# Values and gates of the first 512 tokens behind the first layer's last product

## The chip, the cores and the metric

The program runs on one core of a Trainium2 chip. The metric is the device time of one execution in microseconds. A profile shows the time of each engine: TensorE (PE; its weight loads are PEld), VectorE (DVE), ScalarE (ACT), GpSimd (POOL), and SyncE (SP), whose queue issues the transfers from and to device memory.

## The reference

One layer of an encoder on two sequences, 1024 tokens ("sample") and 512 ("prompt"), width 1024, hidden width 2816, all in float32:

```python
x = x + 0.5 * rmsnorm(swiglu(rmsnorm(x, g0), w1, w3, w2), g1)      # first layer (ffn1), post-norm
h = rmsnorm(x, mix_pre_g)                                          # x / sqrt(mean(x^2) + 1e-6) * g
u = h @ w_in                                                       # 1024 -> 3584 columns
hyena: u[:, :1536], short_conv: up[:L] * w[0] + up[1:L+1] * w[1] + up[2:] * w[2] + b, then two
       long convolutions with filters from hyena_filters() (an MLP with sin over the positions)
retention: q, k = rotary(heads(u[:, 1536:2048])), rotary(heads(u[:, 2048:2560])),
       v = heads(u[:, 2560:3072]), g = u[:, 3072:3584]; silu(g) * rmsnorm(retention(q, k, v))
x = x + rmsnorm(concat(hyena, retention) @ w_out, mix_post_g)
x = x + 0.5 * rmsnorm(swiglu(rmsnorm(x, ...), ...), ...)           # second layer (ffn2)
```

## The kernel before, in words

**Numbers.** A float32 product is made of three matmuls in a rounded format: each operand is split into a high and a low part (hi x hi, hi x lo, lo x hi). `mm3` (L67 to L69) issues the three, `hi_act` (L59) makes a high part on ScalarE as a copy, `lo` (L62) the low part as a difference on the engine that it is given. So each weight block costs a load on SyncE, a high on ScalarE and a low on VectorE or GpSimd before TensorE can use it.

**Stages.** All 1536 tokens lie as columns. `ffn` takes them in two groups of 768, each in two halves (th) of 384. `up_unit` and `down` make the hidden layer and its product by block schemes with fewer products; the weights are loaded as `raw` tiles. At the program's start `normed` loads x in four quads (xq, L192), squares them on ScalarE (L156), sums on VectorE, makes row sums on TensorE (ss, L170 in `rstd3`), the factor r, and spreads it over the partitions by three transposes (rps, L177 in `spread`); only then can the first product start. At the end of each group `post_quads` does the same to the output z: r is spread, z is scaled (L403), the residual is added (L404), z is stored as x1 to device memory, squared and summed, and the row of factors for the next norm goes to device memory (row1, L411).

Behind ffn1 come: `norm_T` (L115), which loads x1 and the row of factors (L122) for 512 tokens, scales (L129) and splits them to hh and hl; `w_in_v` (L813), the values of 512 tokens with four weight chunks (raw2, w2h, w2l), evicted by VectorE (vo, L835); and `w_in_pass` (L774), 24 blocks of 128 columns: 0 to 11 for hyena with the short convolution (its factors are in scw), 12 to 19 queries and keys with rotation, 20 to 23 the gates with silu. It takes tokens 0 to 1023 at once, and beside it `filter_mlp` (products fps, L695) and `filter_taps` (products tapps, L723 and L724; their eviction L725) make the long filters. The values of tokens 512 to 1023 follow, then retention with the last 512 tokens, the long convolutions, the output product and the second layer.

**Order.** `gen_run(main, side, rate)` interleaves two generators in the source. The order on each engine is then set at build time by a planner that simulates the engines (`schedule_with_timeline_sim=True`), so that the program's order is not the source's. A pool hands a buffer out again as soon as its last reader is done. On one engine, and in SyncE's queue, instructions issue in order: what stands behind a waiting one waits too.

The lines that the change replaces: `mix_in_consts` (L840) loads scw and the rotation's tables ahead of the pass; L1235 opens the ffn with its own PSUM pool; the low parts of the first `norm_T`, of `w_in_v` and of `w_in_pass` are made by GpSimd.

## Time and profile before

| | us |
|---|---|
| median of 3 runs | 3313.13 |
| lowest and highest | 3307.2, 3317.64 |
| the profiled execution | 3313.05 |
| its span | 3311.3 |
| TensorE busy in the span | 3068.8 (93%) |
| VectorE busy | 2591.7 (78%) |
| ScalarE busy | 1518.8 (46%) |
| GpSimd busy | 518.1 (16%) |

The profile counts an engine as busy while it executes, not while it waits or issues. A wait is put down to the instruction that came last by its semaphore. The granted clock (PEclk) is TensorE's, as a share of the upper one of its two levels, 1.2 and 2.4 GHz. Transfers run on 16 shared engines, whose mean busy share is the DMA share.

### The profile page before, as it was taken

What the parts mean: (1) busy time and instruction counts of PE and PEld (TensorE: products, weight loads), DVE (VectorE), ACT (ScalarE), POOL (GpSimd) and SP (SyncE); (2) the same over time, 40 slices, a digit from 0 to 9 for tenths busy, and PEclk for the clock granted to TensorE, in tenths of its full rate; (3) what the DMA queues carried; (4) which work ended last, traced back from release to release, by engine and by line L of the source; (5) the groups of instructions that cost most, each with busy time, mean ns of one, the idle gap of its engine ahead of it and who ended that gap; (6) DMA issues with size and microseconds to landing.
All of it is one profiled execution on the core that took longest, in us unless ns stands there. A gap on an engine that the chain in (4) does not pass through costs nothing. (4 is left out here: it accounts for less than half of the span.)

```text
span 3311.3 us, 46272 instructions
## 1 busy us (share of the span) xinstructions
PE 3068.8 (93%) x16764; PEld 2884.0 (87%) x16764; DVE 2591.7 (78%) x4211; ACT 1518.8 (46%) x2588; POOL 518.1 (16%) x380
## 2 busy tenths in 40 slices
PE   5999999999898899989997998896899999999997
PEld 5999999999898677768787887775899999999997
DVE  8888788876786499777676878877889788867776
ACT  6333455433455344457544344455433456433454
POOL 0000000000200322356333534530000000000000
PEclk8999999999999899999998998997899999999998
DMA  3676344422344624444544124465778354322344
GB/s 132 245 297 226 88 151 134 124 71 70 102 118 146 189 105 154 159 168 143 175 115 154 45 85 165 136 200 155 252 262 315 105 150 153 125 74 74 84 130 137
DMA packets 223028, 489.51 MB, mean 148 GB/s; under 512 B 37456, under 2 KB 65488, under 8 KB 220624
## 3 DMA queue, kind: packets, MB, share of 16 engines
q1 hardware_dynamic: 222800, 486.57, 45.1%
q8 instruction: 131, 2.15, 0.3%
q14 instruction: 97, 0.79, 0.1%
HBM read 384.70 MB, written 101.75 MB: 147 GB/s over the span
## 5 line engine op out<-in xcount | busy, mean ns | idle before, releaser
L68 PE MATMUL dn<-xl,w2h 128*128 128x384 f32 x1232 | 416.6, 339 | 6.3 <-DVE xl L62 6.3
L59 ACT ACTIVATE wh<-s 128x512 fp32r<-128x512 f32 x352 | 221.4, 631 | 417.4 <-PE ua L68 115.5
L67 PE MATMUL dn<-xh,w2h 128*128 128x384 f32 x1232 | 404.7, 339 | 0.1
L69 PE MATMUL dn<-xh,w2l 128*128 128x384 f32 x1232 | 403.4, 338 | 0.0
L59 ACT ACTIVATE wh<-raw 128x512 fp32r<-128x512 f32 (+1 forms) x312 | 216.7, 694 | 348.5 <-PE ub L68 92.9
L59 ACT ACTIVATE w2h<-raw 128x512 fp32r<-128x512 f32 (+1 forms) x340 | 228.3, 672 | 301.8 <-PE dn L68 191.7
L62 DVE TENSOR_TENSOR wl<-s,wh 128x512 fp32r<-128x512 f32 x352 | 241.4, 687 | 159.6 <-ACT wh L59 88.2
L95 POOL TENSOR_TENSOR r<-m,mhalf 128x3 f32<-128x3 f32 (+1 forms) x35 | 43.1, 1232 | 1875.9 <-DVE m L94 1874.5
L62 DVE TENSOR_TENSOR w2l<-raw,w2h 128x512 fp32r<-128x512 f32 (+1 forms) x316 | 221.6, 710 | 107.4 <-ACT w2h L59 92.0
L67 PE MATMUL wips<-hh,wh 128*128 128x512 f32 x576 | 233.2, 405 | 15.8 <-DVE vo L835 7.6
L68 PEld LDWEIGHTS dn<-xl,w2h 128*128 128x128 f32 x1232 | 233.1, 189 | 7.1 <-DVE xl L62 7.0
L69 PE MATMUL wips<-hh,wl 128*128 128x512 f32 x576 | 232.6, 404 | 2.2 <-POOL wl L62 2.2
L68 PE MATMUL wips<-hl,wh 128*128 128x512 f32 x576 | 232.4, 404 | 0.5 <-POOL hl L62 0.5
L67 PEld LDWEIGHTS dn<-xh,w2h 128*128 128x128 f32 x1232 | 231.7, 189 | 0.6 <-ACT xh L59 0.4
L69 PEld LDWEIGHTS dn<-xh,w2l 128*128 128x128 f32 x1232 | 232.1, 189 | 0.0
L62 DVE TENSOR_TENSOR wl<-raw,wh 128x512 fp32r<-128x512 f32 (+1 forms) x276 | 196.6, 712 | 24.8 <-ACT wh L59 23.1
L67 PE MATMUL fw<-th,mh 128*128 128x256 f32 x448 | 131.8, 296 | 31.1 <-DVE spec L924 21.0
L67 PEld LDWEIGHTS wips<-hh,wh 128*128 128x128 f32 x576 | 111.5, 194 | 44.4 <-ACT hh L59 11.7
L67 PE MATMUL ub<-t2h,wh 128*128 128x384 f32 x352 | 120.8, 343 | 28.9 <-ACT t2h L59 24.5
L69 PEld LDWEIGHTS wips<-hh,wl 128*128 128x128 f32 x576 | 111.1, 193 | 29.7 <-POOL wl L62 2.9
L68 PEld LDWEIGHTS wips<-hl,wh 128*128 128x128 f32 x576 | 111.4, 193 | 28.0 <-POOL hl L62 1.1
L68 PE MATMUL fw<-tl,mh 128*128 128x256 f32 x448 | 132.5, 296 | 0.3 <-DVE tl L62 0.2
(384 smaller groups left out, 9082.2 us busy)
## 6 DMA issues: line engine op xcount, KB each, us to landing
raw<-ffn_w SPq DMA_DIRECT2D x440, 256.0 KB, 2.7
raw<-ws SPq DMA_DIRECT2D x220, 256.0 KB, 2.7
wsum<-ffn_w SPq DMA_DIRECT2D x60, 768.0 KB, 7.2
raw<-w_in_f SPq DMA_DIRECT2D x48, 512.0 KB, 4.3
ws<-wsum SPq DMA_DIRECT2D x30, 768.0 KB, 6.1
xq<-x SPq DMA_DIRECT2D x16, 768.0 KB, 5.9
res<-x SPq DMA_DIRECT2D x16, 768.0 KB, 6.2
wsum<-ffn_w SPq DMA_DIRECT2D x20, 512.0 KB, 7.0
```

The lines of the kernel that those rows point to most:

```text
L59: self.nc.scalar.activation(hi, src, AF.Copy)
L62: eng.tensor_tensor(lo, src, hi.bitcast(F32), ALU.subtract)
L67: mm(ps, lhsT=ah, rhs=bh, start=first, stop=False, **kw)
L68: mm(ps, lhsT=ah, rhs=bl, start=False, stop=False, **kw)
L69: mm(ps, lhsT=al, rhs=bh, start=False, stop=last, **kw)
L95: nc.gpsimd.tensor_tensor(r, m, self.mhalf[:, :n], ALU.pow)
```

## The change

The values of tokens 0 to 511 are computed right behind the last product of ffn1, and the gates (blocks 20 to 23) of the same tokens behind them; the row sums of the new x1 come among them, later than before. Two of the four weight chunks of the values are loaded and split beside the last product (`first_values`, in quads of pool yq). The PSUM pool of eight banks stays open over ffn1 and these two products. The gates of tokens 512 to 1023 become a pass of their own. The factors of tokens 768 to 1023 are spread over the partitions by two transposes (`spread(r, 2)`) rather than read back from row1. The low parts of these weights and of the norm of tokens 512 to 1023 go from GpSimd to VectorE where the diff says so (`nc.vector`), and the values are evicted by ScalarE. scw becomes a tile of the setup, loaded by `short_consts`, which the ffn calls.

```diff
@@ -81,6 +81,7 @@
         self.gains = self.cp.tile([128, 6, KD], F32, name="gains")
         nc.sync.dma_start(self.gains, self.io["gains"])
+        self.scw = self.cp.tile([128, NHY, 4], F32, name="scw", bufs=1)
...
@@ -112,14 +113,15 @@
-    def norm_T(self, src, g, gi, hp, row, eng=None):
+    def norm_T(self, src, g, gi, hp, row, eng=None, r=None):
 
 
         nc = self.nc
         hh = hp.tile([128, KD, 512], F32R, tag="hh", name="hh")
         hl = hp.tile([128, KD, 512], F32R, tag="hl", name="hl")
-        r = self.np.tile([128, 512], F32, tag="rpre", name="rrow", bufs=1)
-        nc.sync.dma_start(r, row[:, 512 * g:512 * g + 512].broadcast_to([128, 512]))
+        if r is None:
+            r = self.np.tile([128, 512], F32, tag="rpre", name="rrow", bufs=1)
+            nc.sync.dma_start(r, row[:, 512 * g:512 * g + 512].broadcast_to([128, 512]))
...
@@ -170,10 +172,10 @@
-    def spread(self, r):
+    def spread(self, r, n=3):
 
         ps = self.bank("rps")
-        for t in range(3):
+        for t in range(n):
             self.nc.tensor.transpose(ps[:, t * 128:(t + 1) * 128], r[:, t:t + 1].broadcast_to([128, 128]), self.ident)
         return ps
 
@@ -406,11 +408,12 @@
             if row is not None:
                 acc = self.sum_sq([z[0, th], z[1, th]], Y)
                 yield
-                r = self.rstd3(acc)
+                self.row_r = r = self.rstd3(acc)
                 c = 768 * g + 384 * th
                 nc.sync.dma_start(row[:, c:c + 384].rearrange("o (c p) -> (o p) c", p=128), r)
 
-    def ffn(self, n, srcs, dsts, row_in, row_out, X, Y, lead=None):
+    def ffn(self, n, srcs, dsts, row_in, row_out, X, Y, lead=None, extra=()):
@@ -441,7 +444,8 @@
-            self.pm = own.enter_context(pool("pm", 8, space=PSUM))
+            if not extra:
+                self.pm = own.enter_context(pool("pm", 8, space=PSUM))
...
@@ -465,6 +469,8 @@
                 yield from self.weight_sums(w2, Y)
+                if extra:
+                    extra[0]()
@@ -497,6 +503,8 @@
                     for p, c in self.down(w2, hid, Y, z, (1, 4, 7, 2, 3, 5, 6)):
                         if (p, c) == (6, 0):
                             z["sum"] = self.sum_sq([z[0, 1]], Y)
+                        if extra and (p, c) == (3, 0):
+                            extra[1](Y)
                         if p == 6 or (p, c) == (5, 2):
                             run(post_of)
         self.rest = post_of
@@ -771,13 +779,12 @@
-    def w_in_pass(self, hTs, base, gp, rp, wp, psp, d, blks, eng):
+    def w_in_pass(self, hTs, base, gp, rp, wp, psp, d, blks, eng, tag="wi"):
 
         nc = self.nc
         n = len(hTs)
         W = 512 * n
         cols = slice(base, base + W)
-        cos, sin = (self.rope[:, i, :W] for i in range(2))
...
             self.hi_act(wh, raw)
             self.lo(eng, wl, raw, wh)
-            ps = psp.tile([128, W], F32, tag="wi", name="wips")
+            ps = psp.tile([128, W], F32, tag=tag, name="wips")
@@ -801,6 +808,7 @@
                 sw = gp.tile([128, W], F32, tag="c", name="sw")
                 nc.scalar.activation(sw[0:64], ps[64:128], AF.Copy)
                 nc.scalar.activation(sw[64:128], ps[0:64], AF.Copy)
+                cos, sin = (self.rope[:, i, :W] for i in range(2))
                 nc.vector.tensor_tensor(o, ps, cos, ALU.mult)
                 nc.gpsimd.tensor_tensor(sw, sw, sin, ALU.mult)
...
@@ -810,20 +818,38 @@
-    def w_in_v(self, hT, base, n, gp, rp, wp, psp, d, eng):
+    def first_values(self, Y):
+
+        nc = self.nc
+        self.early = []
+        for k2 in range(2):
+            raw, wh, wl = (self.quad(Y, n, t).rearrange("p a b -> p (a b)")[:, :1024].rearrange("p (j c) -> p j c", c=512)
+                           for n, t in (("raw2", F32), ("w2h", F32R), ("w2l", F32R)))
+            nc.sync.dma_start(raw, self.io["w_in_v"][k2])
+            self.hi_act(wh, raw)
+            self.lo(nc.vector, wl, raw, wh)
+            self.early.append((wh, wl))
+
+    def w_in_v(self, hT, base, n, gp, rp, wp, psp, d, eng, banks=False):
 
         nc = self.nc
         hh, hl = hT
         for t0 in range(0, 4, 2 * n):
-            full = [psp.tile([128, 512 * n], F32, tag="wi", name="v") for _ in range(2)]
-            ps = [full[t // n][:, t % n * 512:t % n * 512 + 512] for t in range(2 * n)]
+            if banks:
+                ps = [psp.tile([128, 512], F32, tag="mm", name="v") for _ in range(2 * n)]
+            else:
+                full = [psp.tile([128, 512 * n], F32, tag="wi", name="v") for _ in range(2)]
+                ps = [full[t // n][:, t % n * 512:t % n * 512 + 512] for t in range(2 * n)]
             for k2 in range(4):
-                raw = rp.tile([128, 2, 512], F32, tag="raw", name="raw2")
-                nc.sync.dma_start(raw, self.io["w_in_v"][k2])
-                wh = wp.tile([128, 2, 512], F32R, tag="w", name="w2h")
-                wl = wp.tile([128, 2, 512], F32R, tag="w", name="w2l")
-                self.hi_act(wh, raw)
-                self.lo(eng, wl, raw, wh)
+                if banks and self.early:
+                    wh, wl = self.early.pop(0)
+                else:
+                    raw = rp.tile([128, 2, 512], F32, tag="raw", name="raw2")
+                    nc.sync.dma_start(raw, self.io["w_in_v"][k2])
+                    wh = wp.tile([128, 2, 512], F32R, tag="w", name="w2h")
+                    wl = wp.tile([128, 2, 512], F32R, tag="w", name="w2l")
+                    self.hi_act(wh, raw)
+                    self.lo(eng, wl, raw, wh)
@@ -832,18 +858,19 @@
                 yield
             for t in range(2 * n):
                 o = gp.tile([128, 512], F32, tag="vo", name="vo", bufs=2)
-                nc.vector.tensor_copy(o, ps[t])
+                self.hi_act(o, ps[t])
                 nc.sync.dma_start(d["v"][base // 128 + t0 + t], o)
             yield
 
-    def mix_in_consts(self, gp, rop):
-        nc = self.nc
-        self.rope = rop.tile([128, 2, 1024], F32, name="rope", bufs=1)
-        nc.sync.dma_start(self.rope, self.io["rope"])
-        self.scw = gp.tile([128, NHY, 4], F32, name="scw", bufs=1)
+    def short_consts(self):
+        nc = self.nc
         for i in range(3):
             nc.sync.dma_start(self.scw[:, :, i], self.io["short_w"][i])
         nc.sync.dma_start(self.scw[:, :, 3], self.io["short_b"])
+
+    def mix_in_consts(self, rop):
+        self.rope = rop.tile([128, 2, 1024], F32, name="rope", bufs=1)
+        self.nc.sync.dma_start(self.rope, self.io["rope"])
@@ -1211,23 +1238,36 @@
         with ExitStack() as right:
             e = right.enter_context
             with pool("yq", 20) as Y:
+                pm1 = ExitStack()
+                self.pm = pm1.enter_context(pool("pm", 8, space=PSUM))
                 with pool("xq", 6, side="right") as X, pool("fs", side="right") as self.fs, pool("ft", 6, side="right") as self.ft, \
                         pool("fw", 10, side="right") as self.fw, pool("fr", 5, side="right") as self.fr:
-                    self.ffn(1, xs, x1, None, row1, X, Y)
+                    self.ffn(1, xs, x1, None, row1, X, Y, extra=(self.short_consts, self.first_values))
                 hp = e(pool("hT", side="right"))
-                with pool("xin", 2, side="right") as self.xp, pool("nrm", side="right") as self.np, \
-                        pool("raw", 2, side="right") as raw, pool("w", 4, side="right") as wp, \
-                        pool("gv", 2, side="right") as gp, pool("ft", 6, side="right") as self.ft, \
-                        pool("wv", 2, space=PSUM) as psw, pool("pm", 2, space=PSUM) as self.pm:
+                near = ExitStack()
+                self.xp, self.np = (near.enter_context(pool(n, b, side="right")) for n, b in (("xin", 2), ("nrm", 1)))
+                with pool("gv", 2, side="right") as gp, pool("ft", 6, side="right") as self.ft, \
+                        pool("w", 4, side="right") as wp, pool("raw", 2, side="right") as raw:
                     hTs = [self.norm_T(x1, 0, 2, hp, row1, nc.gpsimd)]
-                    gen_run(self.w_in_v(hTs[0], 0, 2, gp, raw, wp, psw, d, nc.gpsimd), self.rest, 2)
-            with pool("raw", 2) as raw, pool("w", 4) as wp, pool("scw") as gp, pool("rope") as rop:
-                self.mix_in_consts(gp, rop)
-                self.ret_consts(rop)
-                with pool("g", 4) as gp, pool("nrm") as self.np, pool("xin", 2) as self.xp, pool("hT2") as hp2, pool("wi", 2, space=PSUM) as psw, \
+
+                    def main():
+                        yield from self.w_in_v(hTs[0], 0, 2, gp, raw, wp, self.pm, d, nc.vector, banks=True)
+                        yield from self.w_in_pass(hTs, 0, gp, raw, wp, self.pm, d, range(20, 24), nc.vector, tag="mm")
+
+                    rr = self.np.tile([128, 512], F32, tag="rr", name="rrow", bufs=1)
+                    nc.sync.dma_start(rr[:, :256], row1[:, 512:768].broadcast_to([128, 256]))
+                    for i, _ in enumerate(main()):
+                        for _ in range({1: 2, 2: 2, 7: 2}.get(i, 0)):
+                            next(self.rest, None)
+                        if i == 1:
+                            self.hi_act(rr[:, 256:], self.spread(self.row_r, 2)[:, :256])
+                pm1.close()
+            with pool("raw", 2) as raw, pool("w", 4) as wp, pool("rope") as rop:
+                with near, pool("g", 4) as gp, pool("hT2") as hp2, pool("wi", 2, space=PSUM) as psw, \
                         pool("f", 2) as fp, pool("fps", 2, space=PSUM) as psf:
                     hs = [fp.tile([128, 512], F32R, tag=f"h3_{s}", name="h3", bufs=1) for s in range(3)]
-                    hTs.append(self.norm_T(x1, 1, 2, hp2, row1, nc.gpsimd))
+                    hTs.append(self.norm_T(x1, 1, 2, hp2, row1, nc.vector, rr))
+                    self.mix_in_consts(rop)
 
                     def side():
                         yield from self.filter_mlp(fp, psf, hs)
@@ -1237,7 +1277,9 @@
                     hTp = []
 
                     def main():
-                        yield from self.w_in_pass(hTs, 0, gp, raw, wp, psw, d, range(24), nc.gpsimd)
+                        yield from self.w_in_pass(hTs, 0, gp, raw, wp, psw, d, range(20), nc.gpsimd)
+                        yield from self.w_in_pass(hTs[1:], 512, gp, raw, wp, psw, d, range(20, 24), nc.gpsimd)
+                        self.ret_consts(rop)
                         hTp.append(self.norm_T(x1, 2, 2, hp, row1, nc.gpsimd))
                         yield from self.w_in_v(hTs[1], 512, 2, gp, raw, wp, psw, d, nc.gpsimd)
```

SyncE's queue at the program's start, before: constants, two loads of x, five of weights, two of x, nine of weights.

```order
L75 DMA ident<-ident 128x128
L83 DMA gains<-gains 128x48
L192 DMA xq<-x 128x1536 x2
L248 DMA raw<-ffn_w 128x512 x5
L192 DMA xq<-x 128x1536 x2
L248 DMA raw<-ffn_w 128x512 x9
```

The same of the changed kernel, whose lines are numbered a little higher:

```order
L75 DMA ident<-ident 128x128
L83 DMA gains<-gains 128x48
L194 DMA xq<-x 128x1536 x2
L250 DMA raw<-ffn_w 128x512 x5
L868 DMA scw<-short_w 128x12x1 x3
L869 DMA scw<-short_b 128x12x1
L194 DMA xq<-x 128x1536 x2
L250 DMA raw<-ffn_w 128x512 x9
```

The four loads of scw now stand ahead of the second pair of x loads.

TensorE where the last product of ffn1 (dn) ends, before: ss are the row sums of z, rps the spread, v the values.

```order
L68 MATMUL dn<-xl,w2h 128x384
L69 MATMUL dn<-xh,w2l 128x384
L170 MATMUL ss<-ones,acc 128x1 x6
L177 MATMUL rps<-ident,r 128x128 x3
L67 MATMUL v<-w2h,hh 128x512 x2
L68 MATMUL v<-w2l,hh 128x512
L69 MATMUL v<-w2h,hl 128x512
```

The same place of the changed kernel, and below it the rows in which the sums stand:

```order
L68 MATMUL dn<-xl,w2h 128x384
L69 MATMUL dn<-xh,w2l 128x384
L67 MATMUL v<-w2h,hh 128x512
L68 MATMUL v<-w2l,hh 128x512
L69 MATMUL v<-w2h,hl 128x512
L67 MATMUL v<-w2h,hh 128x512
L68 MATMUL v<-w2l,hh 128x512
```

```order
L67 MATMUL v<-w2h,hh 128x512
L68 MATMUL v<-w2l,hh 128x512
L172 MATMUL ss<-ones,acc 128x1 x6
L69 MATMUL v<-w2h,hl 128x512
L67 MATMUL v<-w2h,hh 128x512
```

The six sums come 65 products of the values later than the last dn; behind the 96 of the values come the 96 of the gates.

VectorE at the same place, before: z is scaled and added (not shown, just ahead), squared and summed; then x is normed (L129) and the values are copied out (L835).

```order
L157 TENSOR_TENSOR sq<-sq 128x768
L159 TENSOR_TENSOR sq<-sq 128x384
L160 TENSOR_TENSOR acc<-sq,acc 128x384
L94 TENSOR_SCALAR m<-ss 128x3
L1031 TENSOR_SCALAR nlb<-lg 128x4
L96 TENSOR_TENSOR c<-r 128x3
L97 TENSOR_TENSOR c<-c,m 128x3
L129 SCALAR_TENSOR_TENSOR x<-x,gains,rrow 128x512
```

The changed kernel, from the first low of a weight chunk (wl) on:

```order
L62 TENSOR_TENSOR wl<-raw,wh 128x1024
L131 SCALAR_TENSOR_TENSOR x<-x,gains,rrow 128x512
L405 TENSOR_TENSOR z<-z,rps 128x768 x4
L131 SCALAR_TENSOR_TENSOR x<-x,gains,rrow 128x512 x3
L406 TENSOR_TENSOR z<-z,res 128x768
L62 TENSOR_TENSOR wl<-raw,wh 128x1024
L406 TENSOR_TENSOR z<-z,res 128x768 x3
L62 TENSOR_TENSOR wl<-raw,wh 128x1024
L159 TENSOR_TENSOR sq<-sq 128x768 x2
```

The lows of the weights stand among the norms and the updates of z; the copies of the values are gone from this engine.

## Rows read from the trace of the kernel before

**Rows 1.** The page, part 2: 40 slices of 82.8 us, TensorE and its granted clock.

```profile
PE   5999999999898899989997998896899999999997
PEclk8999999999999899999998998997899999999998
```

**Rows 2.** Busy time by stretch: length, PE, PEld, DVE, ACT, POOL, clock, DMA share, GB/s.

```profile
0.00:40.46 40.46, 7.58 (x31) 6.81 (x31) 29.41 (x41) 22.13 (x32) 2.22 (x8) 0.96 0.40 145
1064.25:1146.14 81.89, 57.47 (x215) 44.94 (x216) 36.30 (x63) 28.40 (x41) 30.10 (x19) 0.79 0.72 204
1146.14:1458.89 312.75, 302.31 (x1266) 241.03 (x1265) 267.52 (x453) 128.26 (x197) 98.44 (x42) 0.98 0.40 142
```

**Rows 3.** TensorE's waits, 1064.25 to 1146.14: total us, times, longest.

```profile
PE wips L67 <- DVE vo L835: 7.6, 1, 7.6
PE ss L170 <- DVE acc L160: 7.2, 1, 7.2
PE wips L67 <- ACT hh L59: 3.3, 1, 3.3
PE wips L69 <- POOL wl L62: 2.2, 1, 2.2
```

**Rows 4.** TensorE in order of time: start, duration, instruction, idle before it.

```profile
1081.71 0.63 PE L69 MATMUL v<-w2h,hl 128*128 128x512 f32 x1
1082.14 0.63 PE L68 MATMUL v<-w2l,hh 128*128 128x512 f32 x1
1144.74 0.39 PE L68 MATMUL wips<-hl,wh 128*128 128x512 f32 x1
1145.91 0.39 PE L67 MATMUL wips<-hh,wh 128*128 128x512 f32 x1
1456.83 0.39 PE L67 MATMUL v<-w2h,hh 128*128 128x512 f32 x1
1458.67 0.39 PE L69 MATMUL v<-w2h,hl 128*128 128x512 f32 x1
```

**Rows 5.** The page, part 5: one low of 512 columns on VectorE.

```profile
L62 DVE TENSOR_TENSOR wl<-s,wh 128x512 fp32r<-128x512 f32 x352 | 241.4, 687 | 159.6 <-ACT wh L59 88.2
```

**Rows 6.** SyncE's queue, the first 20 us, in order of time.

```profile
2.57 2.77 SPq L248 DMA_DIRECT2D raw<-ffn_w  x5
5.39 0.99 SPq L192 DMA_DIRECT2D xq<-x  x2
11.50 51.52 SPq L248 DMA_DIRECT2D raw<-ffn_w  x9
```

**Rows 7.** ScalarE and TensorE at the start; landing of the x loads.

```profile
14.11 1.47 ACT L156 ACTIVATE sq<-xq 128x1536 f32<-128x1536 f32 x1
22.68 1.44 PE L170 MATMUL ss<-ones,acc 128*128 128x1 f32 x6 [6.04 <-DVE acc L160]
30.59 0.90 PE L177 MATMUL rps<-ident,r 128*128 128x128 f32 x3 [5.72 <-DVE r L100]
DMA to landing us min/median/max: 4.4/6.9/9.2
```

**Rows 8.** SyncE's queue from 1086 us on: the short convolution's factors.

```profile
1086.81 9.01 SPq L845 DMA_DIRECT2D scw<-short_w  x3
1095.86 0.84 SPq L846 DMA_DIRECT2D scw<-short_b  x1
```

**Rows 9.** Busy time by stretch of 2 us, with DMA share and GB/s last.

```profile
1094.00:1096.00 2.00, 2.00 (x10) 1.63 (x10) 0.11 (x1) 0.00 (x0) 2.00 (x1) 1.00 1.12 141
1096.00:1098.00 2.00, 2.00 (x11) 1.65 (x10) 0.00 (x0) 0.00 (x0) 1.09 (x2) 1.00 0.64 13
```

**Rows 10.** The filter stage: busy time of 220 us.

```profile
1150.00:1370.00 220.00, 213.45 (x896) 169.81 (x895) 209.41 (x340) 88.10 (x129) 59.58 (x24) 0.98 0.39 139
```

**Rows 11.** TensorE's longest wait, 1146.14 to 1458.89: total, times, longest.

```profile
PE tapps L723 <- DVE tap L725: 6.5, 2, 3.9
```

**Rows 12.** DMA issues, 1080 to 1120: count, KB each, us to landing.

```profile
raw<-w_in_f SPq DMA_DIRECT2D x3, 512.0 KB, 13.5
```

## The prediction, made before the changed kernel ran

> **What bounds the kernel now.** I read the page's slices first. TensorE is over 90% busy in most of the 40, and the reader is to look for where it is not: the first slice, the one around 1064 to 1146 us, where the granted clock falls to 0.7, and the filter stage behind that [rows 1]. So the span is TensorE's time plus its holes, and a change is worth the holes that it closes less those that it opens.
>
> The busy time by stretch prices the holes [rows 2]. The end of the first layer's last product is at 1064.25, the first filter product at 1146.14. Of these 81.89 us TensorE was busy in 57.47, so it was idle for 24.4, and its clock was 0.79. The waits by releaser say what it stood for [rows 3]: 7.2 for the row sums of the post-norm, 7.6 for VectorE's eviction of the values, 3.3 for a high part on ScalarE, 2.2 for a low part on GpSimd, the rest shorter. The timeline gives the pitch of one 512-column matmul: 0.43 us from 1081.71 to 1082.14, at the lower of the two clock levels, and at the upper one 0.234 (five steps from 1144.74 to 1145.91) or 0.23 (eight from 1456.83 to 1458.67) [rows 4]. Each low spell follows one of the long idles.
>
> **The stretch behind the first layer.** It holds 96 value matmuls, 97 of the gates and projections, 18 small sums, 3 spreads and one filter product. At the full pitch this is 96 x 0.23 = 22.1, 97 x 0.234 = 22.7, and for the 22 small ones about 4, by 1.44 for six sums [rows 7]: 48.8. So 57.47 - 48.8 = 8.7 went to the low clock, and with the idle 24.4 the stretch loses 33.1.
>
> The change puts 65 value matmuls directly behind the last down product, ahead of the row sums, since half of their weights are split already in that product's own quads and their input (tokens 0 to 511) was normalized early. 65 x 0.23 = 15.0 us now cover the chain z update, squares, sums, for which TensorE stood 7.2. The wait of 7.6 for VectorE's copies goes because the values have eight separate banks, ScalarE evicts them, and the 96 gate matmuls that follow need only tokens 0 to 511, of which the norm is there. That covers the norm of the next 512 tokens by 96 x 0.234 = 22.5 us. With the holes go the low spells.
>
> What is late next is the split of the remaining weights. VectorE takes over six lows of 1024 columns in the stretch (two of the values, four of the gates) and eight of 512 of the next norm. A low of 512 took 687 ns [rows 5], so twice that, 1.37, bounds the wide one from above and 0.69 from below: 6 x 1.37 + 8 x 0.69 = 13.7 at most. VectorE's load is then 36.3 + 13.7 = 50.0 less four copies, in a stretch of about 52. It sits behind the z updates in program order, so a gate block can come late behind them. The nearest prices are the waits for a low on GpSimd, 2.2, and for a high, 3.3 [rows 3]. No row shows VectorE so full here; in the filter stage it was busy for 209.41 of 220 while TensorE lost 6.55 [rows 10], 3%, or 1.6 of 52. I leave 3 us of loss, the row 3.3 being the nearest; the ends are 0 (the lows hidden by 22.5 us of gates) and 8 (one wait like the 7.6). Gain 33.1 - 3 = 30.1, between 25 and 33.
>
> The factor of tokens 768 to 1023 is spread by two transposes rather than stored and loaded: two spreads at 0.9/3 each [rows 7] are 0.6 us more on TensorE, within the rounding of the 4 above. The four gate blocks are loaded and split twice, 2 MB more; in the stretch the DMA share was 0.72 [rows 2], and ScalarE was busy for 28.4 of 81.9, so I cost it at nothing as long as 96 matmuls cover four loads. If that cover is gone, rival one gives the price.
>
> **The start.** The factors of the short convolution move from 1086.8 to the head of SyncE's queue, behind the first five weight loads and ahead of the second half of the x loads. In the old place they hold the queue for 9.01 + 0.84 = 9.85 us [rows 8], and nobody waits. In the new place everything behind them on SyncE is later: that x pair, issued at 5.39, and the nine weight loads, issued from 11.50 [rows 6]. The x pair is what TensorE waits for: from its landing run ScalarE's squares at 14.11, VectorE's sums, TensorE's six sums at 22.68 and the spread at 30.59, each as the releaser of the next, and the first layer's products only start behind that [rows 7]. TensorE is busy for 7.58 of the first 40.46 us [rows 2], so nothing else covers it, and behind the start TensorE is full: a delay there is paid in whole.
>
> The pair would be issued at 5.39 + 9.85 = 15.24. The slowest landing of an x load in the crowded queue was 9.2, the fastest 4.4 [rows 7]. Before: from 5.39 to about 14.1, where the squares start. After: nothing else is in flight, so 15.24 + 4.4 = 19.6, which is 5.5 later. ScalarE can use the gap for weight parts that it otherwise does later, which takes some off. I take 5. From above the bound is 9.85, the whole hold. From below it is 2: the sums are at 22.68 and their two inputs were 3.9 apart on ScalarE, which late loads landing together would close.
>
> Does a hold of the issuing queue also hold the transfer engines? In the row at 1096 their share was 0.64 while only 13 GB/s moved [rows 9]: small packets keep them busy. The Trainium skill, DMA: Bandwidth & Descriptors, Rules for kernel authors, says that a strided last dimension is lowered to one descriptor per element, and speaks against these loads ahead of anything urgent; its section Bandwidth gives about 10.5 ns per packet, so 6144 elements over 16 engines come to an estimated 4.0 us. By that price the start would lose 4 instead of 5 and the time be 3287. The trace agrees with the rule, and it has the dearer number, 9.85 for the queue.
>
> **The filter stage.** TensorE was busy for 302.31 of 312.75 us [rows 2]. Now the 75 matmuls of the first blocks run ahead of the first filter product, so 75 x 0.234 = 17.5 us less of TensorE's own work lies beside the filter's work on VectorE. At VectorE's 267.52 us [rows 2] and its 209.41/220 = 95% when pressed [rows 10], that work needs 281; the stage shrinks from 312.75 to 295.2. So it still fits, with 14 us to spare, and I take no change. The bounds are -5 (half of the 10.4 idle us go, since what waits now is in part the order at the stage's head) and +15 (four more waits of 3.9 [rows 11]). The blocks 20 to 23 of tokens 512 to 1023 run alone at its end: the same matmuls, four loads and splits more, each under 24 x 0.234 = 5.6 us of matmuls. ScalarE has two table loads fewer; it was busy for 128 of 312.75, so this is off the path.
>
> **Sum.** The profiled run took 3313.05, its span 3311.3, and the median is 3313.13, so no correction is needed. 3313.05 - 30.1 + 5 = 3288. The best ends together give 3313 - 33 + 2 - 5 = 3277, the worst 3313 - 25 + 9.85 + 15 = 3313.
>
> **Rivals.**
> - *A gate block comes late.* A load of a block took 13.5 us to land in this stretch [rows 12], and the queue also carries the stores and loads of x1 that wait for the last z update, ahead of it in order. One idle like the 7.6, and the low clock behind it (8.7 over three spells, 2.9 each), is 10.5: 3288 + 10.5 = 3298. Against it: 13.5 is less than the 15.0 us of value matmuls plus their rest.
> - *VectorE becomes the bound of the filter stage*, and the kernel is slower. The products of the taps come in 16 groups, of which two waited for VectorE, up to 3.9 [rows 11]. VectorE now lies closer to TensorE there. If each of the other 14 waited like that, it would be 14 x 3.9 = 55: 3343. It decides from 35/3.9 = 9 such waits on (3288 + 35 = 3323); with four it is 3303. For it: 95% in 220 us. Against it: the 14 us to spare above.
> - *The start hides the loads*, or the filter stage gains its 5: 3278 to 3283.
>
> **Chances.** The forecast's own case 0.60, with 3281 to 3295, the full price of the start (3293) among it; a late gate block 0.17; VectorE's bound 0.15, of which 0.08 past nine waits; the better case 0.08. About 0.3%, 10 us, is what a measurement can tell from no change, so faster means under 3303 and slower over 3323. Faster: 0.60 + 0.08 + 0.13 of the late block + 0.01 = 0.82. Same: 0.04 + 0.06 = 0.10. Slower 0.08. The range from 3276 to 3304 holds the forecast's case, the better one, and most of the late block.
>
> **What would show it.** In the changed kernel's profile the four factor loads stand at about 5 us on SyncE, the x pair near 15, the six sums near 27 and the first product near 36; nearer to 31 the start cost nothing, near 41 the whole 9.85. No idle lies between the last down product (about 1069) and the first value matmul, and the next fifty us show a granted clock of 1.0 with under 3 us of idle, all for a low on VectorE or a high on ScalarE. The first filter product comes 75 matmuls later in order, near 1139 (1146 - 30 + 5 + 17.5). The taps' waits stay two or three. I am wrong if the waits for a gate block's low exceed 8 us, if the start costs nothing or more than 10, or if the tap products wait in most of their groups.

## The result: 45 us faster, 20 more than forecast

| | us |
|---|---|
| changed kernel, median of 4 runs | 3267.24 (3262.65 to 3269.82) |
| kernel before, beside it | 3311.98 |
| ratio | 0.9861, 95% interval 0.9846 to 0.9876 |
| profiled execution and its span | 3269.82, 3268.0 |

The forecast was 3288, its range 3276 to 3304; the time lies below the range. The direction and the main mechanism were right, the size was not: 25 us were forecast, 45 measured.

First the stretches of the changed kernel, cut at the same places of the program as [rows 2], with the first layer's products as a stretch of their own (length, PE, PEld, DVE, ACT, POOL, clock, DMA share, GB/s):

```profile
0.00:34.29 34.29, 4.14 (x18) 3.69 (x19) 20.55 (x35) 19.70 (x28) 2.22 (x8) 1.00 0.56 164
34.29:1059.23 1024.94, 990.96 (x5604) 985.17 (x5603) 826.29 (x1363) 480.93 (x827) 27.38 (x15) 0.98 0.46 148
1059.23:1130.94 71.71, 66.58 (x292) 53.32 (x291) 39.19 (x69) 31.14 (x47) 7.33 (x6) 0.98 0.66 194
1130.94:1433.84 302.90, 284.42 (x1190) 226.16 (x1191) 284.94 (x467) 130.21 (x203) 107.34 (x43) 0.98 0.43 153
1433.84:1702.60 268.76, 254.83 (x1134) 205.47 (x1133) 206.17 (x242) 166.38 (x271) 136.56 (x115) 0.98 0.52 159
```

The same two stretches of the kernel before that [rows 2] did not show, its first layer's products and its retention stage:

```profile
31.14:1064.25 1033.11, 999.55 (x5603) 992.37 (x5601) 824.57 (x1361) 478.26 (x825) 27.37 (x15) 0.99 0.45 144
1458.89:1737.59 278.70, 259.33 (x1135) 208.62 (x1134) 204.49 (x259) 165.90 (x266) 133.59 (x113) 0.96 0.50 152
```

Read by differences, with 17.5 us for the 75 matmuls that moved ahead of the first filter product:

| stage | forecast | measured, changed less before |
|---|---|---|
| start, to the first product | +5 | 34.29 - 31.14 = +3.2 |
| first layer's products | 0 | 1024.94 - 1033.11 = -8.2 |
| to the first filter product | -30.1 | 71.71 - 17.5 - 81.89 = -27.7 |
| filter stage | 0 | 302.90 + 17.5 - 312.75 = +7.7 |
| retention | 0 | 268.76 - 278.70 = -9.9 |
| all behind it, to the span's end | 0 | 1565.4 - 1573.7 = -8.3 |
| sum | -25.1 | -43.3 |

TensorE's waits in the stretch behind the first layer, those of [rows 3]:

```profile
PE wips L67 <- ACT wh L59: 2.9, 1, 2.9
PE wips L67 <- ACT hh L59: 1.8, 1, 1.8
PE fps L703 <- DVE zs L62: 0.3, 1, 0.3
PE wips L69 <- POOL wl L62: 0.2, 1, 0.2
```

24.4 us of waits became 5.2, and the granted clock went from 0.79 to 0.98. At the seam itself nothing is lost:

```profile
1058.89 0.34 PE L69 MATMUL dn<-xh,w2l 128*128 128x384 f32 x1
1059.06 0.40 PE L67 MATMUL v<-w2h,hh 128*128 128x512 f32 x1
```

The start, which answers to [rows 6, 7]: SyncE's queue, then TensorE.

```profile
5.36 6.16 SPq L868 DMA_DIRECT2D scw<-short_w  x3
11.56 0.84 SPq L869 DMA_DIRECT2D scw<-short_b  x1
12.45 1.48 SPq L194 DMA_DIRECT2D xq<-x  x2
25.84 1.44 PE L172 MATMUL ss<-ones,acc 128*128 128x1 f32 x6 [9.19 <-DVE acc L162]
```

The hold is 7.0 us here and not 9.85, and the sums come 3.16 later.

One thing that the forecast had no term for is in the first layer's products: the same matmuls, in the same order on TensorE but for one neighbouring pair, 8.2 us less. The timeline shows why: the pitch, the time from the start of one matmul to the start of the next, is shorter. The down product of the first group in the kernel before, two rows 225 matmuls apart:

```profile
450.14 0.34 PE L67 MATMUL dn<-xh,w2h 128*128 128x384 f32 x1
...
489.88 0.34 PE L67 MATMUL dn<-xh,w2h 128*128 128x384 f32 x1
```

In the changed kernel, 230 apart, and then its second group's down product, 125 apart:

```profile
450.05 0.34 PE L69 MATMUL dn<-xh,w2l 128*128 128x384 f32 x1
...
489.92 0.34 PE L68 MATMUL dn<-xl,w2h 128*128 128x384 f32 x1
...
952.75 0.34 PE L67 MATMUL dn<-xh,w2h 128*128 128x384 f32 x1
...
974.83 0.34 PE L69 MATMUL dn<-xh,w2l 128*128 128x384 f32 x1
```

39.74/225 = 0.1766 before, 39.87/230 = 0.1733 in the changed kernel, and 22.08/125 = 0.1766 in its second group. The granted clock of these three stretches is 1.00, so this is not the clock gate. In the second layer both kernels run at 0.1734. Over all 5544 products of 384 columns in the first layer, the mean pitch (steps over 0.185 us left out) gives 975.8 us before and 964.6 in the changed kernel, an estimate of 11.2 us; longer spells at a lower clock (0.99 and 0.98 in the two rows) took some of it back.

### The profile page after: what moved, and what is told of

It is laid out like the page before. It is cut to its first block, busy times and chain, and to the rows that moved or that the text cites. A ratio compares the mean times of both kernels' runs of the same rounds, so it can differ in the third digit from the quotient of the medians.

```text
span 3268.0 us, 46298 instructions
## 1 busy us (share of the span) xinstructions
PE 3044.8 (93%) x16766; PEld 2864.0 (88%) x16766; DVE 2621.3 (80%) x4215; ACT 1526.9 (47%) x2607; POOL 507.6 (16%) x368
## 5 line engine op out<-in xcount | busy, mean ns | idle before, releaser
L67 PE MATMUL ub<-t2h,wh 128*128 128x384 f32 x352 | 120.6, 343 | 25.1 <-ACT t2h L59 20.6
L67 PE MATMUL ub<-t4h,wh 128*128 128x384 f32 x352 | 121.2, 344 | 14.9 <-DVE u L279 14.1
```

Source lines behind the costliest of these rows:

```text
L67: mm(ps, lhsT=ah, rhs=bh, start=first, stop=False, **kw)
```

## The experiments

All edits are to the changed kernel (names with a) or the kernel before (with b). "Before" is measured beside each group of runs.

| kernel | median us | before | ratio, 95% interval |
|---|---|---|---|
| b_pad | 3301.89 | 3308.00 | 0.9981 (0.9968 to 0.9994) |
| a_scw_old | 3295.16 | 3308.00 | 0.9957 (0.9944 to 0.9970) |
| a_scw_old_pad | 3283.01 | 3308.00 | 0.9927 (0.9905 to 0.9948) |
| a_pool_lows | 3268.08 | 3308.00 | 0.9873 (0.9853 to 0.9893) |
| a_ralign | 3270.43 | 3310.06 | 0.9876 (0.9858 to 0.9895) |
| b_align | 3295.77 | 3310.06 | 0.9955 (0.9940 to 0.9970) |
| a_row1 | 3272.92 | 3310.06 | 0.9883 (0.9864 to 0.9902) |
| a_no_early | 3277.82 | 3310.06 | 0.9899 (0.9879 to 0.9918) |
| a_right | 3266.79 | 3315.23 | 0.9863 (0.9846 to 0.9881) |
| a_right_scwq | 3273.13 | 3315.23 | 0.9882 (0.9857 to 0.9907) |
| a_gates_back | 3279.84 | 3315.23 | 0.9900 (0.9884 to 0.9915) |
| b_scw | 3305.15 | 3315.23 | 0.9968 (0.9953 to 0.9983) |
| a_late | 3261.38 | 3312.09 | 0.9848 (0.9830 to 0.9865) |
| a_late_right | 3262.31 | 3312.09 | 0.9854 (0.9833 to 0.9874) |
| b_again, a_again | 3318.04, 3270.34 | 3312.09 | one run each |

**Addresses: b_pad, a_scw_old, a_scw_old_pad.** The scw tile in the setup pool takes 192 bytes per partition and moves every pool behind it; the programs of b_pad and of the kernel before are the same, instruction by instruction, but for addresses, and so are those of a_scw_old and a_scw_old_pad.

```diff
+        self.nc_pad = self.cp.tile([128, 48], F32, name="pad", bufs=1)          # b_pad, a_scw_old_pad
-        self.scw = self.cp.tile([128, NHY, 4], F32, name="scw", bufs=1)         # a_scw_old, a_scw_old_pad
+        with ... pool("scw") as sw ...: self.scw = sw.tile(...); self.short_consts()   # behind mix_in_consts
```

> The kernel before with nothing but an unused tile of 192 bytes per partition in the setup pool, so that all pools behind it lie 192 bytes higher, as in the changed kernel; no instruction differs. Theory 'address': this shift is what brought the pitch of the first layer's matmuls from 0.176 to 0.1735 us in the changed kernel; then the first layer is 8 to 13 us shorter here too and the median about 3300 to 3304. Rival 'chance': the pitch belongs to the single execution or to the chip and not to the kernel; then the median stays within 3 us of the kernel before (3312), and the pitch may be either.

> The changed kernel with the four short-convolution factors loaded as before, in a pool of their own at the rotation's tables; so no loads at the head of SyncE's queue, and the pools back at the old addresses. The six sums return from 25.84 to 22.7 us: 3.15 us are gained at the start. Theory 'address': the first layer's pitch returns to 0.176 and costs 8 to 13 us: 3272 to 3277. Rival 'chance': no change of the pitch, 3264.

> The same with the unused tile of 192 bytes per partition, so with the addresses of the changed kernel. Both theories: only the start differs from the changed kernel, by -3.15 us: 3264. 'Address' wants it 8 to 13 us under the run without the tile, 'chance' wants both alike within 3.

"Address" holds. b_pad's first layer took 1025.4 us, a_scw_old's 1034.4 with a pitch of 0.1766, a_scw_old_pad's 1026.3. The first down product of b_pad, 229 matmuls apart, so 39.69/229 = 0.1733:

```profile
450.14 0.34 PE L68 MATMUL dn<-xl,w2h 128*128 128x384 f32 x1
...
489.83 0.33 PE L68 MATMUL dn<-xl,w2h 128*128 128x384 f32 x1
```

By the medians the shift is worth 6 us on the kernel before and 12 on the changed one. Both theories were wrong on the level: 3264 was expected for a_scw_old_pad, and it took 3283. With the loads of the factors in their old place the new order took 16 us more (22 by the ratios). The stretch behind the first layer took 82.9 us against 71.7, and TensorE's waits in a_scw_old_pad show the place:

```profile
PE wips L67 <- ACT wh L59: 17.7, 3, 14.3
```

and SyncE's queue of the same kernel the reason:

```profile
1098.57 4.95 SPq L868 DMA_DIRECT2D scw<-short_w  x3
...
1106.79 0.57 SPq L869 DMA_DIRECT2D scw<-short_b  x1
1107.45 2.60 SPq L413 DMA_DIRECT2D row<-r  x1
1110.10 1.30 SPq L790 DMA_DIRECT2D raw<-w_in_f  x2
```

The next weight blocks are issued behind the factors, at 1110.10; the changed kernel issues the same two at 1100.10. Of these 10 us the factors hold the queue for 5.5. The rest are the x loads and the row, which the planner put ahead of the weights in this program, so the 16 us are the price of the place together with the order that came with it. In the kernel before TensorE stood for other things at that point [rows 3]; what the old place cost there is read from b_scw below.

**Lows: a_pool_lows.** `nc.vector` back to `nc.gpsimd` in three calls.

```diff
-wp, self.pm, d, nc.vector, banks=True)    range(20, 24), nc.vector, tag="mm")    row1, nc.vector, rr)
+wp, self.pm, d, nc.gpsimd, banks=True)    range(20, 24), nc.gpsimd, tag="mm")    row1, nc.gpsimd, rr)
```

> The changed kernel with the low parts of the first values, the first gates and the norm of tokens 512 to 1023 by GpSimd again. Theory: GpSimd takes 2.4 us for what VectorE does in at most 1.4, and the value and gate matmuls wait for it as before (2 to 4 us, with the low clock behind it); the filter stage gains nothing since its lows were few: 3272 to 3277. Rival: VectorE's fuller load is what made the filter stage 7.7 us longer in the changed kernel, and relieving it of up to 14 us gives that back: 3259 to 3263.

3268.08: neither. The stretch took 73.0 us, the filter stage 304.9, so the filter stage's 7.7 us do not come from these lows. By the medians it makes no difference which engine makes them. This does not price the lows alone: the planner gave the rest of the program another order, and up to the retention's end the profile is 2 to 5 us longer than the two of the changed kernel, while the output product's stage took 176.9 us where they had 186.3 and 185.1.

**Which distance counts: a_ralign, b_align, a_right.** An unused tile at SBUF's upper end, which moves the pools allocated from there (weights and xq in the first layer).

```diff
             e = right.enter_context
+            e(pool("rpad", side="right")).tile([128, 24], F32, name="rpad", bufs=1)   # a_right: 56
```

> The changed kernel with an unused tile of 96 bytes per partition at the upper end of SBUF, so that the pools allocated from there lie on multiples of 128 bytes like those from the lower end; no instruction differs. Theory 'offset': a matmul whose weights and moving tile have the same address modulo 128 runs at the shorter pitch, others at the longer one or at either. Then the second down product goes from 0.1767 to 0.1733 us (1848 matmuls, -6.1 us) and the products of the pass over the first 512 tokens from 0.233 to 0.228 (989, -5 us): 3267 - 11 = 3256, at most 3260. Rival: the offset decides nothing by itself, the pitch changes by chance at a fall of the clock: 3267 within 3.

> The kernel before with two unused tiles, 64 bytes per partition in the setup and 96 at the upper end, so that the first layer's weights and moving tiles all lie on multiples of 128 bytes. 'Offset': about 3790 matmuls of the first layer go from 0.1767 to 0.1733 (-12.5 us) and 1020 of the pass from 0.234 to 0.228 (-6): 3308 - 18 = 3290, the first layer near 1021 us. Rival: nothing beyond what 192 bytes gave, 3302.

> The changed kernel with an unused tile of 224 bytes per partition at the upper end of SBUF: now the weights and the moving tiles of the first layer and of the pass have the same address modulo 256 everywhere; no instruction differs. Theory 'modulo 256' (from the runs so far: 0 apart gives 0.1733 and 0.228 us, 32 apart either, 96 to 224 apart 0.176 and 0.233): the down products all go to 0.1733 (3696 matmuls, 1.6 ns each on the mean, -6 us) and the products with hT from 0.233 to 0.228 (about 1000 in the pass and 400 behind it, -5 to -7): 3267 - 12 = 3255, the first layer's products near 1019 us. Rival 'modulo 128' is out by the run with 96 bytes; rival 'hidden': VectorE sets the pass, so only the first layer gains: 3261.

128 bytes is not the measure: where the difference became 128 (a_ralign), the first layer's products ran at 0.1760. Taken over the profiles, by the difference of the moving tile's and the weights' address modulo 256 in the built programs:

| difference | 384 columns | 512 columns |
|---|---|---|
| 0 | 0.1734; in the kernel before, among products at 96, 0.1744 | 0.2276 (a_right) to 0.2285 (b_align); the retention's own products 0.230 |
| 32 | 0.1733; a down product also 0.1767 | 0.233 |
| 64 | | 0.229 to 0.232 |
| 96 | 0.1766 (before) | 0.233 |
| 128 | 0.1760 (a_ralign) | 0.2325 |
| 160, 192, 224 | | 0.234, 0.233, 0.233 |

It is the difference that counts here and not the address itself: with both at 0, at 64 or at 128 modulo 256 the second layer ran at 0.1734 alike. One kernel has both pitches side by side, from one stage: in b_align the two halves of the pass over 1024 tokens alternate, one at 0 (the first 24 matmuls here, 5.46/24 = 0.2275), one at 192 (the next 23 steps, 5.37/23 = 0.2335):

```profile
1384.17 0.39 PE L67 MATMUL wips<-hh,wh 128*128 128x512 f32 x1
...
1389.63 0.39 PE L67 MATMUL wips<-hh,wh 128*128 128x512 f32 x1
...
1395.00 0.39 PE L69 MATMUL wips<-hh,wl 128*128 128x512 f32 x1
```

One place doesn't fit: the retention's own products ran at 0.230 at 0 in most kernels, and at 0.228 in a_right. In a_right the pitch is the short one throughout the first layer and the pass; its second down product, 213 matmuls apart:

```profile
953.07 0.33 PE L67 MATMUL dn<-xh,w2h 128*128 128x384 f32 x1
...
989.99 0.33 PE L67 MATMUL dn<-xh,w2h 128*128 128x384 f32 x1
```

36.92/213 = 0.1733. Yet the time is the changed kernel's, 3266.8: "modulo 256" is right on the pitch and wrong on the time. Part of that is a miscount in the expectations: the first layer has 1848 down products in both groups together, about half of them in the second, so 1848 x 1.6 ns = 3 us were to be had and not 6; the 6.1 named for a_ralign is twice too high in the same way. The first layer took 1022.8 us, 2.2 less. In the filter stage TensorE was busy for 1.8 us less and idle for 3.1 more, and it waited for VectorE at the taps 6 times, 11.4 us in all, where the changed kernel did so 5 times, 9.6 us; the stage took 304.3 against 302.9. That VectorE sets the time there is what the rival 'hidden' held, though its 3261 was not met either. b_align gave 14 of the 18 us (1024.0 in the first layer).

**The other parts, one at a time: a_row1, a_no_early, a_gates_back.**

```diff
+nc.sync.dma_start(rr, row1[:, 512:1024].broadcast_to([128, 512]))          # a_row1, for spread and its copy
+extra=(self.short_consts, lambda Y: None)), self.early = []                # a_no_early
-yield from self.w_in_pass(hTs, 0, ..., range(20, 24), nc.vector, tag="mm") # a_gates_back; range(24) in the pass
```

> The changed kernel with the factors of tokens 512 to 1023 all loaded from the stored row again, not spread on the chip. Theory: the gates of the first 512 tokens cover the way through memory, so it is worth nothing: 3267 within 3. Rival: the norm of the second 512 comes late and TensorE waits for its high part (3.3 us before, and a low clock behind it): 3272 to 3276.

> The changed kernel without the early load and split of the first two weight chunks of the values; they are loaded behind the first layer's own tiles. Theory: TensorE stands behind the last down product for a load (4.3 us), a high (1.3) and a low (1.4), 7 us, and pays some 3 us of low clock: 3275 to 3278. Rival: the chunks are ready anyway, since their buffers are free before the last product ends: 3267.

> The changed kernel with the gates of the first 512 tokens back in the pass (24 blocks over 1024 tokens, no gates behind the values, no weights loaded twice). Theory: nothing covers the norm of the second 512 tokens, TensorE waits for it as before (the 7.6 and 3.3 us of the kernel before) with the low clock behind: 3277 to 3283. Rival: the gates are not needed as cover, since the values alone cover the sums, and the second loads and the longer filter stage (+7.7 us) are saved: 3260 to 3265.

a_row1 cost 5.7 us by the medians, and its interval overlaps that of the changed kernel; in its profile the stretch took 81.8 us against 71.7. TensorE waits once for a gate's low, because VectorE stands in order behind the norm, whose factor is still on its way through memory:

```profile
PE wips L69 <- DVE wl L62: 9.2, 1, 9.2
```

a_no_early cost 10.6, a_gates_back 12.6, the sizes that their first theories gave, but not the waits. Behind the last down product a_no_early stands for 3.4 us (1.5 for a high, 1.9 for a low) and not 7, at a granted clock of 0.96; where the rest goes was not found. Without the gates the sums themselves wait 12.5 us on VectorE, and a high costs 5.0. As with the lows, the planner gave each of these three another order behind the edit (the output product's stage took 177 us in a_row1 and a_gates_back), so the medians price the edit with its order.

**The factors' place: b_scw, a_right_scwq, a_late, a_late_right.** b_scw moves them alone; a_right_scwq is a_right with `nc.gpsimd.dma_start`; a_late ties them to the second down product, a_late_right adds the 224 bytes.

```diff
+                            self.hi_act(self.scw, z[0, 0][:, 0, :48].rearrange("p (a b) -> p a b", b=4))
+                            self.short_consts()
                             extra[1](Y)
```

> The kernel before with the short convolution's factors alone moved: their tile into the setup, their loads to the head of SyncE's queue, as in the changed kernel. Theory 'nobody waits for them in the old place': the start loses 3.15 us, the addresses give the 6 us that 192 bytes gave: 3308 - 6 + 3 = 3305. Rival 'they delay the loads behind them in the old place too': the stretch behind the first layer gives 5 to 11 us more: 3294 to 3300.

> The same, with the four loads of the short convolution's factors issued by GpSimd at the start and not by SyncE. Theory: what the start lost is SyncE's hold; the six sums return from 25.84 to 22.7 us and the kernel is 3.1 us faster than the run with the tile alone: 3252. Rival: the small packets themselves slow the x loads on the shared transfer engines, half of the loss or all stays: 3253 to 3255.

> The changed kernel with the factors' four loads tied to the second group's down product: ScalarE first writes the tile from z, then SyncE loads it, among that product's weights. Theory 'place': the start is back at 22.7 us for the six sums, the down product hides the loads, 3.2 us gained: 3264. Rival: the loads hold the queue in front of the weights there too, and TensorE waits for them: 3267 to 3275.

> The same with the unused tile of 224 bytes at the upper end, so with equal addresses modulo 256. If 'place' holds and the even pitch is worth its 2 us in the first layer beside it: 3261 to 3263. If VectorE and the loads pace what the pitch frees: as the run without the tile, within 2.

b_scw: 10 us under the kernel before beside it, where 192 bytes alone gave 6 and the start took 3.7; its stretch behind the first layer took 79.0 us against 81.9. So the old place had cost the kernel before a few us too, at the edge of what was measured. a_right_scwq gained nothing: the first product came at 34.4 us. The queue was free, the x pair was issued at 5.52, but the first six sums moved from 15 to 18.3 and the second stayed at 25.9: the small packets themselves delay the x loads. a_late shows "place":

```profile
23.18 1.44 PE L172 MATMUL ss<-ones,acc 128*128 128x1 f32 x6 [6.05 <-DVE acc L162]
```

2.7 us of the start are back, and with 3261.4 it is the fastest version, 6 us under the changed kernel by the medians; the two intervals overlap. Nothing waits for the factors beside the down product. Of the rest, 2.8 us are the first layer (1022.1 us): at the difference of 32 all its down products ran at the shorter pitch in this profile, though the edit moves no address. So the even addresses had nothing left to give (3262.3, first layer 1021.5).

**A second profile: b_again, a_again.** No edit.

> The kernel before, profiled a second time. If the stages behind the gates differ by the execution, the long convolutions (331.1 us) and the rest from the output product's end (1044.5) come out up to 4 us shorter each; if by the kernel, they stay within 1. The first layer's pitch stays at 0.176 (1033 us) if the addresses set it.

> The changed kernel, profiled a second time. By the execution: the same stages (327.0 and 1041.2) differ by up to 4 us from the first profile. By the kernel: within 1. The first layer near 1025, the stretch to the first filter product near 72.

The kernel before again:

```profile
31.49:1068.86 1037.37, 1003.43 (x5603) 997.72 (x5601) 824.84 (x1361) 479.20 (x825) 27.35 (x15) 0.98 0.45 143
1068.86:1151.52 82.66, 57.67 (x215) 45.03 (x215) 35.97 (x63) 28.38 (x40) 30.53 (x19) 0.79 0.71 202
```

and the changed one:

```profile
34.92:1065.19 1030.27, 996.11 (x5604) 990.62 (x5603) 827.25 (x1363) 479.91 (x827) 27.37 (x15) 0.98 0.45 147
1065.19:1136.44 71.25, 65.05 (x292) 52.17 (x291) 39.44 (x69) 31.26 (x47) 7.34 (x6) 1.00 0.66 195
```

The stretch repeats within 1 us, and the first layer's difference nearly so (7.1 after 8.2), but both layers are 4 to 5 us longer, and in the changed kernel both groups' down products now ran at 0.1766. At the difference of 32 the first layer took from 1022.1 to 1031.1 us in ten profiles, so a median of four runs can be off by a few us for that alone. The long convolutions were 331.1 and 326.2 us before, 327.0 and 327.6 in the changed kernel: their 4 us belong to the execution. The rest from the output product's end was 1044.5 and 1044.6 before, 1041.2 and 1038.6 changed, and lay between 1038 and 1045 over all eighteen profiles (to TensorE's last instruction), so that its 3 to 6 us stay open.

## Why the prediction fell short

- *The stretch behind the first layer.* Right: 27.7 of 30.1, with 5.2 us of waits where 3 were left. What was late next was a weight block's high part (2.9, a load) and the norm's (1.8), not a low on VectorE. VectorE's lows took 12.5 us, as counted; its whole load was 39.2 and not 50, since the copies and the first short convolution fell out, and it is spread over 71.7 us, with the 75 matmuls behind the gates.
- *The parts of it.* The spread of the factor was costed at 0.6 us and nothing gained; taken back, it costs 10 us of this stretch and 5.7 by the medians. The cover that the text gave to the gates and to the early weights was real: 12.6 and 10.6 by the medians.
- *The factors' old place, "and nobody waits".* Nearly true of the old order (b_scw: some 3 us of the stretch). In the new one the hold stands in front of the weights that TensorE needs next, 16 us by the medians with the order that came with it. The sum did not suffer, since it took the stretch as a whole, but the move to the front, read as a pure cost of 5, gave more than it took.
- *The start.* 3.2 for 5: the term was sized by the hold of 9.85 [rows 8] and was 7.0 in an empty queue. The lower bound of 2 was nearer. The estimate of 4.0 worked out from the Trainium skill, DMA: Bandwidth & Descriptors, Bandwidth, came nearer than the row of another place. That is luck in part: the page's figure is for the 64 packets of one copy issued from GpSimd, and the division by 16 engines is the prediction's own. a_right_scwq shows that the packets and not only the queue delay the x loads.
- *The filter stage.* "It still fits" was too kind: VectorE was busy for 285 of 302.9 us (94%), and the stage lost 7.7, inside the bounds of -5 to +15. All of it is idle time of TensorE, 18.5 us after 10.4, and the sign named for it, two or three waits at the taps, was passed (against [rows 11]):

```profile
PE tapps L731 <- DVE tap L733: 9.6, 5, 3.4
```

- *The stage behind it*, retention, had no term and gave 9.9 back: in its first 41 us TensorE was idle for 10.3 before and for 7.1 of 40 in the changed kernel, at a clock of 0.83 and 0.92. In the second profiles the two stages took 312.7 and 283.6 before, 302.8 and 267.4 changed. So together they gained 2.3 and 8.6 us on equal work. Which edit does this was not told apart.
- *The step that failed:* the sum has terms for the start, the stretch behind the first layer and the filter stage, and puts everything else at nothing without a reason. In the first layer the order on TensorE is the same indeed; the addresses are not. A tile of 192 bytes in the setup pool, which the diff shows and the prediction read as a move of loads, moved the first layer's tiles against their weights and shortened its pitch: 8.2 us in the first profile, 6 (before) and 12 (changed) by the medians of the runs that isolate it. The other part of the miss lies behind the filter stage, -9.9 in retention and -8.3 from there to the end; of the -8.3, 4 belong to the execution, and the cause of what is left of both stays open.

## What to carry to other kernels

When a change moves a tile into an early pool, all that is allocated behind it moves too: compare the pitch of the same matmuls in both profiles before a difference is given to the edit. A queue's hold is costed by what stands behind it in the new order, not by who waited in the old one. A stretch of TensorE's holes is best closed by work whose inputs are ready at its start, and then each small round trip in it (here a factor through memory, 10 us of the stretch) shows. A small edit can also bring another planned order far behind it: compare the stages that the edit does not touch before its price is read from a median.

## What the runs showed of the hardware

The pitch of a matmul depended on the address of its moving tile against that of its weights: 0.1733 us for 384 columns and 0.2276 for 512 where both were equal modulo 256 bytes, 0.1760 to 0.1767 and 0.2325 to 0.234 at differences of 96 to 224, at a granted clock of 1.00 in both. In b_align the two halves of one stage ran at 0.2275 and 0.2335 side by side. The retention's own products do not fit (0.230 at 0). At a difference of 32 a down product ran at either pitch, and changed between two profiles of one program. A shorter pitch did not always shorten the time: where VectorE was busy for 94% of a stage, 1.8 us less of TensorE's time came with 3.1 us more of its idle time, and the stage was no shorter (a_right). Three loads of 6 KB in small packets held SyncE's queue for 9.01, 6.16 and 4.95 us in three places, and delayed other loads also when another engine issued them.
